# Hyena filter: two factors folded as one tile, stored by one transfer, all steps beside the first mixture's experts

## Chip, cores, metric

The kernel runs on one core of one Trainium2 chip. The metric is the device time of one execution in microseconds (us), taken as the median of several executions. Engines: PE (TensorE, matrix products), DVE (VectorE), ACT (ScalarE), POOL (GpSimd), SP (SyncE, which only issues transfers). Each engine takes its instructions strictly in the order in which they stand in its own program.

## What is computed

Two transformer blocks on 1024 tokens of width 1024. The first ends in a mixture of 32 experts. The second has a linear recurrence and a Hyena convolution side by side, and ends in a mixture of 16 experts. The filter of the Hyena convolution depends on weights alone and not on the tokens:

```python
h = jnp.sin(freq[0] * (z @ w1 + b1)); h = jnp.sin(freq[1] * (h @ w2 + b2))
h = (h @ w3).reshape(L, HYENA_ORDER, 2, HYENA_WIDTH)
filt = h * jnp.exp(-t * deltas[None, :])[:, None, None, :]
...
for n, gate in enumerate((x1, x2)):
    k = bidir_kernel(filt[:, n, 0], filt[:, n, 1])     # length 2L
    z = gate * fftconv(z, k, filt_bias[l, n])          # rfft(k) times rfft(z)
```

The kernel needs the spectrum of `k` for both orders `n` and all 1024 channels. It splits the transform of length 2L into two real halves, made from the sum and the difference of the two directions of the filter. These are the two factors, numbered `s` = 0, 1.

## The kernel before

The program runs in stages: first block (0 to about 700 us of the profiled execution), its mixture `moe1` (to about 1505), the start of the second block `start2` (to about 1585), the recurrence, the Hyena convolution, the output projections (to about 2790), the second mixture `moe2` (to the end). Code between stages is ordered ahead of time by a scheduler that may move an instruction past others of its engine; the rows below that show an order come from its result.

**moe1** (L731) runs 32 experts. Each needs six slabs of 1 MB of weights: `slab` (L643) loads one into one of four buffers `raw`, ACT rounds it to `hi` (L43), DVE subtracts to get `lo` (L44), and PE multiplies three times (L50 to L52: `hi*xh`, `lo*xh`, `hi*xl`). Every third expert multiplies its second matrix unsplit (L690, `rawn`). `fetch` gathers tokens `xg` by a POOL transfer (L634), `add` scales the result on ACT into `ys` (L740) and adds it to `h_d` in memory by a POOL transfer (L741). After each slab the function `tick` runs, 192 times in all, and each tick takes one step of the generator `fill`: that is the Hyena filter, put between the experts' instructions.

**filter_steps** (L964) has 16 rounds, one for each order `n` and each group `cg` of 128 channels, of 13 steps each, and one step ahead of them: 209. A round loads weights `W` through POOL (L983), forms sum and difference on POOL (L989, L990), splits them, multiplies with `H` on PE into `ps` (L1000, L1001), and DVE multiplies with the decay into `X0` and `X1`, one tile for each factor (L1002). Then for each factor in turn `fold_pairs` (L841) makes four `leaf` tiles on DVE by adds and subtracts (L847 to L863, 18 instructions), PE multiplies each with a constant `F` into `ks` (L1023), ACT copies `ks` to `kv` (L1029) after every second leaf, and POOL stores `kv` in `K_d` (L1031), 512 KB in runs of 512 bytes. `kv`, `ks` and `ps` have one buffer each, so the first copy into `kv` of a factor waits until the store of the factor before it has landed.

Ticks end before the steps do. The 17 steps that are left are taken up by the second block (`fl`, L1345); the scheduler puts their instructions into `start2`.

**start2** (L1149) loads eight row tiles `x` of the first block's result from `h_d` (L1156), five buffers of them (`XB`, L1116), squares and sums each twice on ACT (L1167, the second time after a product with `gf` on DVE, L1166), forms scales for four tiles at once, normalises to `n` (L1170), writes `x` times a scale to `x_d` (L1171 to L1173), transposes on PE (L92) and splits into `hTh` and `hTl`. With the first four tiles done, PE may multiply the first halves of two projections (L50 to L52 on `ps`, weights `whi` and `wlo` of a tile `wraw` loaded at L1125); the second halves need all eight tiles. From there on PE is busy nearly all the time through the recurrence.

Of the kernel before, what the change touches and what calls it, by code (L numbers as in the profile page):

```python
# [11 lines left out]
F32=mybir.dt.float32; F32R=mybir.dt.float32r; I32=mybir.dt.int32; U32=mybir.dt.uint32  # L12
AF=mybir.ActivationFunctionType; ALU=mybir.AluOpType; AX=mybir.AxisListType
PSUM=bass.MemoryType.PSUM; DRAM=bass.MemoryType.DRAM
# [65 lines left out]
def flat(ap):  # L80
    return ap.rearrange("p a b -> p (a b)")
# [372 lines left out]
CAP=96  # L454
# [275 lines left out]

def moe1(k,a,R,fill):  # L731

# [6 lines left out]
    def add(p,y,gate,idx):  # L739
        ys=p.tile([128,1024],F32,name="ys")[0:CAP]; nc.scalar.activation(ys,flat(y)[0:CAP],AF.Copy,scale=gate[0:CAP])  # L740
        nc.gpsimd.indirect_dma_start(out=acc_d,out_offset=bass.IndirectOffsetOnAxis(ap=idx[0:CAP],axis=0),in_=ys,in_offset=None,compute_op=ALU.add)  # L741
    with ExitStack() as es:
        wraw,whl,p=moe_pools(tc,es,2,"m1")
        R.route()
        ph,pt,py=psums(es,2)
        U=Unit(k,p,(ph,pt,py),wraw,whl,CAP)
        more=R.beyond(ph); k.gathers=[]
        def tick():
            if next(more,0)==0 and not U.wnat: U.wnat=es.enter_context(tc.tile_pool(name="m1x",bufs=2))
            next(fill,None)  # L750
        U.tick=tick; U.early=EARLY1
        ys_={}
        def unit(b):
            def down(h):
                ys_[b]=py.tile([128,2,512],F32,name="y")
                U.down(h,w2[b],ys_[b],True,True)
            def fin():
                add(p,ys_.pop(b),R.gw[:,b:b+1],R.tok[:,b:b+1])
            return dict(fetch=lambda: U.fetch(xn_d,R.tok[:,b:b+1]),up=lambda x: U.up(x,w1[b],w3[b],NAT(b)),down=down,fin=fin)
        us=[unit(b) for b in range(32)]  # L760
        run_units(U,us,2)

    nov=nc.values_load(R.nov[0:1,0:1],min_val=0,max_val=NB-32)
# [199 lines left out]
FC=128  # L963
def filter_steps(k,a,H_d,K_d,KN_d,p,pp):  # L964


    nc=k.nc
# [7 lines left out]
    for cg in range(1024//C):  # L975
# [3 lines left out]
        for n in range(2):  # L979
# [13 lines left out]
            yield  # L993
            Xs=[p.tile([128,8,C],F32,name=f"X{s}") for s in range(2)]
            for i in range(4):
                ps=pp.tile([128,2,2,C],F32,name="ps")
                for j in range(2):
                    t=2*i+j
                    with k.tc.issue_after(k.routed_pe.ins) if cg==n==t==0 else nullcontext():
                        nc.tensor.matmul(ps[:,j],H[:,128*t:128*t+128],Wh[:,0:2],start=True,stop=False)  # L1000
                    nc.tensor.matmul(ps[:,j],H[:,128*t:128*t+128],Wl[:,0:2],start=False,stop=True)  # L1001
                for s in range(2): nc.vector.tensor_tensor(Xs[s][:,2*i:2*i+2],ps[:,:,s],dec[:,2*i:2*i+2],op=ALU.mult)  # L1002
                if i%2: yield
# [4 lines left out]
            nc.tensor.matmul(ps[0:1,0],H[:,0:1],Wl[:,2],start=False,stop=True)  # L1008
            for s in range(2): nc.vector.tensor_tensor(Xs[s][0:1,0],ps[0:1,0],dec[0:1,0],op=ALU.mult)
            nc.vector.tensor_tensor(Xs[0][0:1,0],Xs[0][0:1,0],br,op=ALU.add)  # L1010
            for s in range(2):
                X=Xs[s]
                kv=p.tile([128,8,C],F32,name="kv")
                fold=fold_pairs(nc,p,X,C)
                nx=next(fold)
                yield
                for _ in range(4):
                    b,o=nx
                    nx=next(fold,None)
                    if b%4==0: ks=pp.tile([128,4,C],F32,name="ks")  # L1020
                    for j in range(2):
                        for q in range(2):
                            nc.tensor.matmul(ks[:,b%4+j],F[:,b+j,q,128*s:128*s+128],o[:,j,q],start=q==0,stop=q==1)  # L1023
                    if s==0 and b==0:
                        ps=pp.tile([128,4,C],F32,name="ps")
                        for q in range(2): nc.tensor.matmul(ps[0:1,0],FN[:,q:q+1],o[:,0,q],start=q==0,stop=q==1)
                        kn=p.tile([1,C],F32,name="kn"); nc.vector.tensor_copy(kn,ps[0:1,0])
                        nc.gpsimd.dma_start(KN_d[n,cg:cg+1],kn)
                    if b%4: nc.scalar.activation(kv[:,b-2:b+2],ks,AF.Copy)  # L1029
                    if b<6: yield  # L1030
                nc.gpsimd.dma_start(K_d[n,cg,:,:,s],kv)  # L1031
                yield
# [82 lines left out]
NPRE=3  # L1115
XB=5  # L1116

# [489 lines left out]
def net(tc, a, c, out):  # L1607
    k=K(); k.tc=tc; k.nc=tc.nc; k.c=c; nc=tc.nc
    with tc.tile_pool(name="const",bufs=1) as pc, tc.tile_pool(name="dram",bufs=1,space=DRAM) as k.dram:
# [8 lines left out]
        with tc.tile_pool(name="rt1",bufs=1) as po:  # L1618
# [5 lines left out]
            R,vec=k.R,k.vec  # L1624
            fl=filter_steps(k,a,H_d,K_d,KN_d,fls.enter_context(tc.tile_pool(name="fl",bufs=1,side="right")),fls.enter_context(tc.tile_pool(name="flp",bufs=1,space=PSUM)))
            moe1(k,a,R,fl)
        R,rt=block2(k,a,vec,h_d,K_d,KN_d,fl,fls.close,dict(x2=x2_d,ga=ga_d,sg=sg_d,ma=ma_d,z=z_d,x3=x3_d,xn2=xn2_d))
        moe2(k,a,R,out)
# [29 lines left out]
```

## Time and profile before

| | us |
|---|---|
| median of 3 runs | 3951.88 (3943.78 to 3955.34) |
| profiled execution, device time | 3954.99 |
| its span from first to last instruction | 3953.2 |
| busy: PE, DVE, ACT, POOL | 3707.7, 3079.9, 2215.5, 445.9 |
| mean granted clock of TensorE | 0.969 of full speed |

A view by windows gives the busy time of each engine in a stretch, with the granted clock (1.00 is 2.4 GHz, 0.50 is 1.2 GHz), the share of time in which the 16 DMA engines had a packet, and the rate. A timeline lists instructions with start, duration, engine, line, output and inputs, and in brackets how long the engine sat idle before and what it was then released by. PEld is the loading of weights into TensorE, which runs beside the products. Products overlap: 512 columns are issued every 0.23 us at the full clock, though one lasts 0.39.

### The profile page before, as it was taken

Reading aid. Unit: us, or ns where it says so; the run is one execution under the profiler, and the core shown is the slowest. Engines: PE = TensorE matmul, PEld = TensorE weight load, DVE = VectorE, ACT = ScalarE, POOL = GpSimd, SP = SyncE. Lnnn points to the kernel's source line nnn. Section 1 sums busy time; section 2 is a strip of 40 time slices with the busy share of each in tenths; the row PEclk is TensorE's granted clock in tenths of the full one; section 3 lists DMA queues with packets and bytes.
Section 4 is the critical chain, followed back from the end, with each engine's and each line's share of the span. In section 5 each row is a group of like instructions: output and inputs, shape, how many; then the busy total and the mean of one; then the engine's idle time right before and its main releaser. Section 6 shows DMA issues by size and latency. Waiting matters only on the chain.

```text
span 3953.2 us, 49738 instructions
## 1 busy us (share of the span) xinstructions
PE 3707.7 (94%) x18392; PEld 2955.4 (75%) x18392; DVE 3079.9 (78%) x4728; ACT 2215.5 (56%) x2522; POOL 445.9 (11%) x469
## 2 busy tenths in 40 slices
PE   8999898899989996999999999999699999999997
PEld 6787676577666674777888887877587778777785
DVE  3655765799888897676889999743788888888887
ACT  3733653566566664785333334222477777777776
POOL 0013000322333221100000000000000010100100
PEclk9999899899999997999999999999799999999998
DMA  3234635899989994122333335644799999999997
GB/s 97 67 94 110 168 98 177 279 333 317 312 289 305 321 297 144 58 84 85 102 96 107 110 105 157 201 139 170 259 373 378 374 367 380 368 373 375 366 383 297
DMA packets 459240, 900.99 MB, mean 228 GB/s; under 512 B 41734, under 2 KB 140257, under 8 KB 458610
## 3 DMA queue, kind: packets, MB, share of 16 engines
q1 hardware_dynamic: 414578, 801.90, 58.3%
q0 software_dynamic: 42832, 92.21, 8.5%
q10 hardware_dynamic: 1584, 3.67, 0.3%
q8 instruction: 146, 2.39, 0.3%
q14 instruction: 100, 0.82, 0.1%
HBM read 795.27 MB, written 102.29 MB: 227 GB/s over the span
## 4 chain that ended last, share of the span: by engine, by line
PE 60%; DVE 8%; issue 5%; ACT 5%; DMA 5%; POOL 1%; DVEq 0%; ACTq 0%; POOLq 0%; SPq 0%
PE h L51 7%; PE h L52 7%; PE h L50 7%; PE ps L51 5%; PE ps L52 5%; PE ps L50 5%; PE y L51 4%; PE y L52 3%; PE y L50 3%; PE iv L1086 3%; DVE lo L44 2%; DMA raw<-in_expert_w 2%; PE ks L1023 1%; PE U L1074 1%; PE y L690 1%
## 5 line engine op out<-in xcount | busy, mean ns | idle before, releaser
L44 DVE TENSOR_TENSOR lo<-raw,hi 128x2048 fp32r<-128x2048 f32 x551 | 1250.3, 2287 | 148.7 <-ACT hi L43 148.0
L43 ACT ACTIVATE hi<-raw 128x2048 fp32r<-128x2048 f32 x551 | 1047.9, 1913 | 210.7 <-PE h L52 114.3
L51 PE MATMUL h<-lo,xh 128*128 128x512 f32 (+1 forms) x1536 | 612.0, 398 | 14.2 <-DVE lo L44 13.5
L50 PE MATMUL h<-hi,xh 128*128 128x512 f32 (+1 forms) x1536 | 611.7, 399 | 0.7 <-ACT xh L43 0.7
L52 PE MATMUL h<-hi,xl 128*128 128x512 f32 (+1 forms) x1536 | 603.9, 393 | 0.0
L50 PE MATMUL ps<-hTh,whi 128*128 128x512 f32 x896 | 359.4, 402 | 3.3 <-ACT ge L1252 2.8
L51 PE MATMUL ps<-hTl,whi 128*128 128x512 f32 x896 | 355.3, 397 | 0.0
L52 PE MATMUL ps<-hTh,wlo 128*128 128x512 f32 x896 | 354.4, 396 | 0.0
L51 PEld LDWEIGHTS h<-lo,xh 128*128 128x128 f32 (+1 forms) x1536 | 276.8, 180 | 103.3 <-DVE lo L44 36.2
L52 PEld LDWEIGHTS h<-hi,xl 128*128 128x128 f32 (+1 forms) x1536 | 276.3, 180 | 71.4 <-issue 1.4
L50 PEld LDWEIGHTS h<-hi,xh 128*128 128x128 f32 (+1 forms) x1536 | 276.8, 180 | 69.9 <-ACT xh L43 1.2
L51 PE MATMUL y<-lo,hh 128*128 128x512 f32 (+1 forms) x680 | 272.0, 400 | 0.4 <-DVE lo L44 0.4
L50 PE MATMUL y<-hi,hh 128*128 128x512 f32 (+1 forms) x680 | 267.8, 394 | 0.3 <-ACT hi L43 0.3
L52 PE MATMUL y<-hi,hl 128*128 128x512 f32 (+1 forms) x680 | 266.8, 392 | 0.0
L44 DVE TENSOR_TENSOR wlo<-wraw,whi 128x1024 fp32r<-128x1024 f32 x96 | 117.2, 1221 | 131.7 <-ACT whi L43 104.4
L634 POOL DMA_INDIRECT xg<-xn_d,tok x48 | 101.5, 2115 | 862.0 <-issue 780.8
L50 PEld LDWEIGHTS ps<-hTh,whi 128*128 128x128 f32 x896 | 170.8, 191 | 37.3 <-ACT ge L1252 3.3
L52 PEld LDWEIGHTS ps<-hTh,wlo 128*128 128x128 f32 x896 | 170.4, 190 | 35.6
L51 PEld LDWEIGHTS ps<-hTl,whi 128*128 128x128 f32 x896 | 171.3, 191 | 33.3 <-DVE hTl L44 0.5
L43 ACT ACTIVATE whi<-wraw 128x1024 fp32r<-128x1024 f32 x96 | 101.4, 1056 | 161.2 <-PE ps L51 154.4
L1023 PEld LDWEIGHTS ks<-leaf,F 128*128 128x128 f32 x1024 | 139.0, 201 | 65.5 <-ACT kv L1029 30.5
L1023 PE MATMUL ks<-leaf,F 128*128 128x128 f32 x1024 | 145.0, 287 | 41.3 <-ACT kv L1029 26.3
(615 smaller groups left out, 7108.7 us busy)
## 6 DMA issues: line engine op xcount, KB each, us to landing
raw<-in_expert_w SPq DMA_DIRECT2D x170, 1024.0 KB
raw<-in_w_down SPq DMA_DIRECT2D x128, 1024.0 KB
raw<-in_w_up SPq DMA_DIRECT2D x127, 1024.0 KB
raw<-in_w_gate SPq DMA_DIRECT2D x126, 1024.0 KB
wraw<-in_w_in SPq DMA_DIRECT2D x80, 512.0 KB
K<-K_d SPq DMA_DIRECT2D x256, 128.0 KB
rawn<-in_expert_w SPq DMA_DIRECT2D x22, 1024.0 KB
K_d<-kv POOLq DMA_DIRECT2D x32, 512.0 KB, 6.9
```

The costliest lines, as they stand in the source:

```text
L43: nc.scalar.activation(hi, src, AF.Copy)
L44: (eng or nc.vector).tensor_tensor(lo, src, hi.bitcast(F32), op=ALU.subtract)
L50: nc.tensor.matmul(ps, sh, mh, start=start, stop=False)
L51: nc.tensor.matmul(ps, sh, ml, start=False, stop=False)
L52: nc.tensor.matmul(ps, sl, mh, start=False, stop=stop)
L634: s.k.gathers.append(s.k.nc.gpsimd.indirect_dma_start(out=xg,out_offset=None,in_=src_d,in_offset=bass.IndirectOffsetOnAxis(ap=idx[0:s.m],a ...
L690: for n in range(2): nc.tensor.matmul(y[0:s.m,n],hh[:,f],raw[:,j,512*n:512*n+512],start=first and f==0,stop=last and f==3)
L1023: nc.tensor.matmul(ks[:,b%4+j],F[:,b+j,q,128*s:128*s+128],o[:,j,q],start=q==0,stop=q==1)
L1074: for q in range(2): nc.tensor.matmul(U[:,j,q],F[:,2*(b+j)+q],um[:,j,q],start=True,stop=True)
L1086: for i in range(2): nc.tensor.matmul(iv[:,j,q].rearrange("p a t -> p (a t)"),Y[i][:,j,q],G[:,2*(b+j)+q,i],start=i==0,stop=i==1)
```

## The change

Both factors become halves of one tile `X` of twice the width, are folded by one call of `fold_pairs`, and each leaf's products for both factors go to one `ks`, copied to `kv` at once; one transfer of 1 MB, 8 KB for each partition, stores a round. A round has 8 steps instead of 13. `moe1` spreads all 129 steps over its first 190 ticks, so nothing is left for the second block. `ys` of the first mixture has one buffer instead of two; the row tiles of `start2` have eight instead of five; the folding has a pool of its own (`folds`).

```diff
 def add(p,y,gate,idx):
-        ys=p.tile([128,1024],F32,name="ys")[0:CAP]; nc.scalar.activation(ys,flat(y)[0:CAP],AF.Copy,scale=gate[0:CAP])
+        ys=p.tile([128,1024],F32,name="ys",bufs=1)[0:CAP]; nc.scalar.activation(ys,flat(y)[0:CAP],AF.Copy,scale=gate[0:CAP])
...
+        due=[0,0]
         def tick():
...
-            next(fill,None)
+            due[0]+=1
+            while due[1]*190<due[0]*nfill: next(fill,None); due[1]+=1
...
         run_units(U,us,2)
+        for _ in fill: pass
...
-            Xs=[p.tile([128,8,C],F32,name=f"X{s}") for s in range(2)]
+            X=p.tile([128,8,2,C],F32,name="X")
...
-                for s in range(2): nc.vector.tensor_tensor(Xs[s][:,2*i:2*i+2],ps[:,:,s],dec[:,2*i:2*i+2],op=ALU.mult)
+                nc.vector.tensor_tensor(X[:,2*i:2*i+2],ps,dec[:,2*i:2*i+2,None,:].to_broadcast([128,2,2,C]),op=ALU.mult)
...
-            for s in range(2):
-                X=Xs[s]
-                kv=p.tile([128,8,C],F32,name="kv")
-                fold=fold_pairs(nc,p,X,C)
...
-                    if b%4: nc.scalar.activation(kv[:,b-2:b+2],ks,AF.Copy)
-                    if b<6: yield
-                nc.gpsimd.dma_start(K_d[n,cg,:,:,s],kv)
+            kv=p.tile([128,8,2,C],F32,name="kv")
+            fold=fold_pairs(nc,folds(),X.rearrange("p t s c -> p t (s c)"),2*C)
+            nx=next(fold)
+            yield
+            for _ in range(4):
+                b,o=nx
+                nx=next(fold,None)
+                ks=pp.tile([128,2,2,C],F32,name="ks")
+                for j in range(2):
+                    for s in range(2):
                         for q in range(2):
+                            nc.tensor.matmul(ks[:,j,s],F[:,b+j,q,128*s:128*s+128],o[:,j,q,C*s:C*s+C],start=q==0,stop=q==1)
...
+                nc.scalar.activation(kv[:,b:b+2],ks,AF.Copy)
+                if b==6: nc.gpsimd.dma_start(K_d[n,cg],kv)
                 yield
...
-XB=5
+XB=8
...
-            moe1(k,a,R,fl)
-        R,rt=block2(k,a,vec,h_d,K_d,KN_d,fl,fls.close,dict(x2=x2_d,ga=ga_d,sg=sg_d,ma=ma_d,z=z_d,x3=x3_d,xn2=xn2_d))
+            moe1(k,a,R,fl,FSTEPS,lambda: ff.append(fls.enter_context(tc.tile_pool(name="flf",bufs=1,side="right"))))
+        fls.close()
+        R,rt=block2(k,a,vec,h_d,K_d,KN_d,iter(()),lambda: None,dict(x2=x2_d,ga=ga_d,sg=sg_d,ma=ma_d,z=z_d,x3=x3_d,xn2=xn2_d))
```

Three places in the engines' orders show what moves.

POOL in the middle of moe1. Before, one round of the filter has two stores `K_d<-kv`, with the gather `xg`, the addition to `h_d` and other rounds' `W` between them:

```order
L1031 DMA K_d_74<-kv_8538 1024x1x128
L741 DMA h_d_62<-ys_8756,tok_3840 1152x1024
L634 DMA xg_8985<-xn_d_63,tok_3840 96x1024
L1031 DMA K_d_74<-kv_8720 1024x1x128
L741 DMA h_d_62<-ys_8982,tok_3840 1152x1024
L634 DMA xg_9174<-xn_d_63,tok_3840 96x1024
L984 DMA br_9341<-in_filt_bias_2 1x16x8
L1028 DMA KN_d_75<-kn_9067 16x1x8
L1031 DMA K_d_74<-kv_9028 1024x1x128
```

After, at about the same place, two stores stand a whole round apart, each of 2048 numbers for a partition:

```order
L1035 DMA K_d_74<-kv_8281 128x2048
L995 TENSOR_TENSOR W_8910<-W_8910 128x128
L996 TENSOR_TENSOR W_8910<-W_8910 128x128
L741 DMA h_d_62<-ys_8628,tok_3840 1152x1024
L634 DMA xg_8844<-xn_d_63,tok_3840 96x1024
L990 DMA br_8911<-in_filt_bias_2 1x16x8
L1033 DMA KN_d_75<-kn_8736 16x1x8
L741 DMA h_d_62<-ys_8841,tok_3840 1152x1024
L989 DMA W_9294<-in_filt_w3_2 64x2x128
L634 DMA xg_9011<-xn_d_63,tok_3840 96x1024
L1035 DMA K_d_74<-kv_8674 128x2048
```

The store of the first factor is gone from between the factors; one remains for a round.

PE from the end of moe1 into start2. Before, products of the filter's last round stand behind the end of the mixture and ahead of the first transposes (L92):

```order
L1001 MATMUL ps_14857<-Wl_14439,H_6080 128x256
L1007 MATMUL ks_15051<-Wh_14438,H_6080 1x128
L1008 MATMUL ks_15051<-Wl_14439,H_6080 1x128
L1023 MATMUL ks_15070<-leaf_15061,F_6074 128x128 x4
L1026 MATMUL ps_15075<-leaf_15061,FN_6076 1x128 x2
L1023 MATMUL ks_15070<-leaf_15067,F_6074 128x128 x4
L1023 MATMUL ks_15102<-leaf_15086,F_6074 128x128 x4
L1023 MATMUL ks_15102<-leaf_15099,F_6074 128x128 x4
L1023 MATMUL ks_15126<-leaf_15117,F_6074 128x128 x4
L1023 MATMUL ks_15126<-leaf_15123,F_6074 128x128 x4
L92 MATMUL ps_13074<-ident_60,n_13070 128x128 x4
```

After, the transposes follow the mixture's last product and its loop at once:

```order
L52 MATMUL y_12565<-hi_12586,hl_12562 96x512
L773 REGISTER_ALU
L773 COMPARE_AND_BRANCH
L773 UNCONDITIONAL_BRANCH
L92 MATMUL ps_12716<-ident_60,n_12712 128x128 x4
```

The filter's products have moved ahead of the end of the mixture, among the experts' products.

SP at the start of start2. Before, the last three row tiles stand behind four weight tiles:

```order
L769 UNCONDITIONAL_BRANCH
L1156 DMA x<-h_d 128x1024 x4
L1125 DMA wraw<-in_w_in 128x8x128 x2
L1156 DMA x<-h_d 128x1024
L1125 DMA wraw<-in_w_in 128x8x128 x2
L1156 DMA x<-h_d 128x1024 x3
L1125 DMA wraw<-in_w_in 128x8x128 x4
```

After:

```order
L773 UNCONDITIONAL_BRANCH
L1160 DMA x<-h_d 128x1024 x4
L1129 DMA wraw<-in_w_in 128x8x128 x2
L1160 DMA x<-h_d 128x1024 x4
L1129 DMA wraw<-in_w_in 128x8x128 x6
```

All eight row tiles are now issued ahead of the third weight tile. From the first half projection on, the order of every engine is the same in both kernels.

## Rows read from the trace of the kernel before

**Rows 1.** Windows: stretch, length, busy us (instructions) by engine, PEclk, DMA share, GB/s.

```profile
745.00:1500.00 755.00, 717.59 (x3720) 515.44 (x3719) 658.44 (x981) 462.09 (x453) 221.16 (x177) 0.97 0.92 303
...
1508.00:1583.00 75.00, 41.90 (x192) 33.37 (x193) 54.13 (x113) 39.96 (x67) 13.44 (x26) 0.72 0.53 172
```

**Rows 2.** Waits of PE, 745 to 1505: us in total, times, longest.

```profile
PE ks L1023 <- ACT kv L1029: 23.3, 6, 9.0
```

**Rows 3.** Timeline in moe1: start, duration, instruction, idle before and releaser.

```profile
1123.60 10.05 POOL L634 DMA_INDIRECT xg<-xn_d,tok  x1 [0.30 <-issue]
1133.65 1.00 POOL L1031 DMA_DIRECT2D K_d<-kv  x1
1140.58 0.60 ACT L1029 ACTIVATE kv<-ks 128x512 f32<-128x512 f32 x1 [9.45 <-DMA K_d<-kv]
1141.23 2.08 PE L1023 MATMUL ks<-leaf,F 128*128 128x128 f32 x8 [8.43 <-ACT kv L1029]
...
1254.46 2.07 PE L1023 MATMUL ks<-leaf,F 128*128 128x128 f32 x8 [8.95 <-ACT kv L1029]
```

**Rows 4.** View of the tile K_d, its stores: time from issue to landing.

```profile
DMA to landing us min/median/max: 3.8/6.9/9.9
```

**Rows 5.** Windows behind three of the stalls, columns as in rows 1.

```profile
1030.00:1040.00 10.00, 9.96 (x40) 7.65 (x41) 4.77 (x6) 4.18 (x3) 0.00 (x0) 0.71 1.04 319
1140.00:1150.00 10.00, 8.77 (x31) 5.22 (x32) 2.76 (x2) 3.48 (x4) 1.05 (x3) 0.75 0.25 79
1250.00:1260.00 10.00, 5.54 (x24) 4.66 (x25) 2.76 (x2) 3.89 (x4) 1.59 (x1) 0.62 0.52 139
```

**Rows 6.** Groups on PE, 1499.8 to 1550: count, busy us, mean ns, idle before.

```profile
L1023 PE MATMUL ks<-leaf,F 128*128 128x128 f32 x96 | 17.1, 342 | 18.5 <-DVE leaf L863 10.1 <-DVE leaf L849 4.6 <-ACT kv L1029 3.6
```

**Rows 7.** Chain that ended last, 1440 to 1660: start, share in us, piece.

```profile
1486.86 0.89 PE ks L1023 x8
1487.75 0.53 PE ps L1026 x4
```

**Rows 8.** Waits of all engines, 800 to 1500.

```profile
POOL K_d L1031 <- ACT kv L1029: 93.6, 15, 12.2
...
ACT hi L43 <- DMA raw<-in_expert_w: 36.0, 18, 3.9
```

**Rows 9.** Timeline in start2, SP, ACT, DVE and PE, as in rows 3.

```profile
1507.86 2.07 SPq L1156 DMA_DIRECT2D x<-h_d  x4
1524.45 1.06 ACT L43 ACTIVATE whi<-wraw 128x1024 fp32r<-128x1024 f32 x1 [5.44 <-DMA wraw<-in_w_in]
1543.33 1.28 DVE L1170 SCALAR_TENSOR_TENSOR n<-x,rby,gm 128x1024 f32<-128x1024 f32 x1
1548.71 7.61 SPq L1156 DMA_DIRECT2D x<-h_d  x3
1569.45 1.29 DVE L1170 SCALAR_TENSOR_TENSOR n<-x,rby,gm 128x1024 f32<-128x1024 f32 x1
1582.47 1.22 PE L50 MATMUL ps<-hTh,whi 128*128 128x512 f32 x2
```

**Rows 10.** Groups on DVE by shape, 1508 to 1550, columns as in rows 6.

```profile
L1166 DVE TENSOR_TENSOR x<-x,gf 128x1024 f32<-128x1024 f32 x5 | 6.1, 1221 | 1.3 <-ACT junk L1167 0.8 <-issue 0.5
L44 DVE TENSOR_TENSOR hTl<-ps,hTh 128x512 fp32r<-128x512 f32 x3 | 2.0, 684 | 0.0
```

**Rows 11.** Groups on DVE by shape, 745 to 1507: the folding.

```profile
L858 DVE SCALAR_TENSOR_TENSOR S<-DE,X 128x512 f32<-128x512 f32 x59 | 40.0, 678 | 0.1
L861 DVE SCALAR_TENSOR_TENSOR UW<-S 128x128 f32<-128x128 f32 x118 | 28.6, 279 | 0.2
```

**Rows 12.** View of the line of the addition to h_d: issue to landing.

```profile
DMA to landing us min/median/max: 5.4/8.6/14.7
```

**Rows 13.** Timeline of one such addition and the next ys, as in rows 3.

```profile
1118.45 4.85 POOL L741 DMA_INDIRECT h_d<-ys,tok  x1 [3.86 <-ACT ys L740]
1150.64 1.11 ACT L740 ACTIVATE ys<-y,gw 96x1024 f32<-96x1024 f32 x1 [1.12 <-PE y L690]
```

More of the change, by code (lines that the diff above doesn't have):

```diff
@@ L729, in moe_pools, with moe1 @@
     return e(name=pre+"r",bufs=nr if nb>1 else 2),e(name=pre+"w",bufs=3*SPL if nb>1 else 2*SPL),e(name=pre,bufs=nb)
-def moe1(k,a,R,fill):
+def moe1(k,a,R,fill,nfill,folds):
     tc,nc=k.tc,k.nc
@@ L746, in moe1 @@
         U=Unit(k,p,(ph,pt,py),wraw,whl,CAP)
+        folds()
+        due=[0,0]
         more=R.beyond(ph); k.gathers=[]
@@ L963, with filter_steps @@
 FC=128
-def filter_steps(k,a,H_d,K_d,KN_d,p,pp):
+FSTEPS=1+16*8
+def filter_steps(k,a,H_d,K_d,KN_d,p,pp,folds):
     nc=k.nc
@@ L1008, in filter_steps @@
             nc.tensor.matmul(ps[0:1,0],H[:,0:1],Wl[:,2],start=False,stop=True)
-            for s in range(2): nc.vector.tensor_tensor(Xs[s][0:1,0],ps[0:1,0],dec[0:1,0],op=ALU.mult)
-            nc.vector.tensor_tensor(Xs[0][0:1,0],Xs[0][0:1,0],br,op=ALU.add)
-            for s in range(2):
-                X=Xs[s]
-                kv=p.tile([128,8,C],F32,name="kv")
-                fold=fold_pairs(nc,p,X,C)
[L1015 to L1021, printed above, removed]
-                        for q in range(2):
[L1023 to L1028, printed above, removed]
-                    if b%4: nc.scalar.activation(kv[:,b-2:b+2],ks,AF.Copy)
-                    if b<6: yield
-                nc.gpsimd.dma_start(K_d[n,cg,:,:,s],kv)
@@ new lines, in filter_steps @@
+            for s in range(2): nc.vector.tensor_tensor(X[0:1,0,s],ps[0:1,0],dec[0:1,0],op=ALU.mult)
+            nc.vector.tensor_tensor(X[0:1,0,0],X[0:1,0,0],br,op=ALU.add)
+            kv=p.tile([128,8,2,C],F32,name="kv")
[8 more added lines that the diff above has]
+                    for s in range(2):
+                        for q in range(2):
+                            nc.tensor.matmul(ks[:,j,s],F[:,b+j,q,128*s:128*s+128],o[:,j,q,C*s:C*s+C],start=q==0,stop=q==1)
+                if b==0:
+                    ps=pp.tile([128,4,C],F32,name="ps")
+                    for q in range(2): nc.tensor.matmul(ps[0:1,0],FN[:,q:q+1],o[:,0,q,0:C],start=q==0,stop=q==1)
+                    kn=p.tile([1,C],F32,name="kn"); nc.vector.tensor_copy(kn,ps[0:1,0])
+                    nc.gpsimd.dma_start(KN_d[n,cg:cg+1],kn)
+                nc.scalar.activation(kv[:,b:b+2],ks,AF.Copy)
+                if b==6: nc.gpsimd.dma_start(K_d[n,cg],kv)
@@ L1624, in net @@
             R,vec=k.R,k.vec
-            fl=filter_steps(k,a,H_d,K_d,KN_d,fls.enter_context(tc.tile_pool(name="fl",bufs=1,side="right")),fls.enter_context(tc.tile_pool(name="flp",bufs=1,space=PSUM)))
-            moe1(k,a,R,fl)
-        R,rt=block2(k,a,vec,h_d,K_d,KN_d,fl,fls.close,dict(x2=x2_d,ga=ga_d,sg=sg_d,ma=ma_d,z=z_d,x3=x3_d,xn2=xn2_d))
+            ff=[]
+            fl=filter_steps(k,a,H_d,K_d,KN_d,fls.enter_context(tc.tile_pool(name="fl",bufs=1,side="right")),fls.enter_context(tc.tile_pool(name="flp",bufs=1,space=PSUM)),lambda: ff[0])
+            moe1(k,a,R,fl,FSTEPS,lambda: ff.append(fls.enter_context(tc.tile_pool(name="flf",bufs=1,side="right"))))
+        fls.close()
+        R,rt=block2(k,a,vec,h_d,K_d,KN_d,iter(()),lambda: None,dict(x2=x2_d,ga=ga_d,sg=sg_d,ma=ma_d,z=z_d,x3=x3_d,xn2=xn2_d))
         moe2(k,a,R,out)
```

## Prediction

> **What bounds the kernel now.** I read the windows first, then the waits of PE, then single stalls in the timeline. In the first mixture, from 745 to 1500 us, PE is busy for 717.6 of 755 us and DVE for 658.4 [rows 1]: PE sets the pace, so what PE is given or spared there moves the end, and DVE, 13% idle, does not. Of the 37.4 us in which PE stands still there (755 - 717.6), 23.3 belong to one wait, the products `ks` waiting for ACT's copy `kv` of the products before them [rows 2]. The reader is to see that this is no slow copy. At 1141 PE has stood still for 8.43 us, ACT for 9.45, and ACT was released by a transfer: the store of `kv` to `K_d`, which POOL had issued at 1133.65, since a gather of 10.05 us was ahead of it in POOL's queue; at 1254 the same, with 8.95 us [rows 3]. The store of the first factor has to land before the second factor may use `kv`, and landing takes 6.9 us at the median [rows 4]. Behind three of the stalls the granted clock is 0.71, 0.75 and 0.62 in the next 10 us [rows 5], that is, part of them at the lower level of 1.2 GHz, though PE is at work again.
>
> From 1508 to 1583 nothing is a full bound: PE is busy for 41.9 of 75 us, DVE for 54.1, ACT for 40.0 [rows 1]. It is a chain of loads, sums, scales and transposes with the rest of the filter in between. From 1582 PE runs steadily, so the start of the second half projection at 1582.47 [rows 9] is the point to watch: all that comes behind it is ordered alike in both kernels and moves with it.
>
> **The change part by part.** First, the wait for the store between the factors goes. After the change the store is issued behind the last of a round's four leaves, and the next copy into `kv` belongs to the first leaf of the next round. By the order of PE's products, at 0.23 us for each of 512 columns, 20 to 27 us of other products lie between the two, against 2 to 6 before. Even a store that POOL issues 10 us late and that lands in 9.9 us, the longest [rows 3, 4], fits. So I take the whole wait out, 23.3 us [rows 2]. Bounds: 0 to 23.3.
>
> Second, the clock behind the stalls. At a granted clock c, a stretch with PE busy for b holds b x (1 - c) us too many: 9.96 x 0.29 + 8.77 x 0.25 + 5.54 x 0.38 = 2.9 + 2.2 + 2.1 = 7.2 us [rows 5]. If PE does not stop, this goes too. Bounds: 0 to 7.2.
>
> Third, PE's work that is moved into the mixture. Behind 1500 stand 96 passes of `ks` [rows 6]; eight take 0.89 us at the full clock [rows 7], so 96 take 10.7. With them go 14 products of `H` with 256 columns (half of the 0.23 us for 512, 1.7 us in all) and four passes with `FN`, 0.53 us [rows 7]. PE is the bound there, so all 12.9 us count. There is no cover for them.
>
> Fourth, the wider instructions of DVE. 128 numbers take 0.279 us, 512 take 0.678 [rows 11], so a number costs 0.00104 us and an instruction 0.146 beside. A round drops 22 instructions (4 of the decay, 18 of the folding), 3.2 us by this price, some 50 us in 16 rounds; less the last round that moves in (about 15 us of DVE), DVE is relieved by 35 us of 658. I credit nothing, as DVE is not the bound. If it shortened PE's other 14 us of standing still, the end would come up to 14 us earlier: that is the lower bound. `kv` keeps four copies of 512 numbers a round, so ACT has the same work.
>
> Fifth, the weights. PE's stalls let the four weight buffers fill. ACT still waits for weights 18 times, 36.0 us in all [rows 8], so the transfers are near their limit: 303 GB/s at a DMA share of 0.92 [rows 1]. A shorter mixture asks for about 2% more each second. I charge 3 us, between 0 and 17 (all that the first three parts gain). The stores carry the same bytes; that a store now writes 8 KB in one run is left uncredited.
>
> Sum of the mixture: -23.3 - 7.2 + 12.9 + 3 = -14.6 us.
>
> Sixth, `start2`. Time 0 is SP's issue of the row tiles, 1507.86 [rows 9]. The first normalisation comes at 1543.33. ACT, in order, sat 5.44 us for the first weight tile until 1524.45 [rows 9], and this stays; what leaves are the filter's copies on ACT and its folds on DVE behind it. Going through ACT's and DVE's new orders with the durations of before, from 1524.45: roundings and squares of 1.06 us [rows 9] (one width, 1024 numbers), products of 1.22 [rows 10], and an estimate of 4 us for the column instructions, I get the first normalisation at 1539.7, 3.6 us earlier. The second group of four then starts at 1569.45 in the trace, 26.1 us after the first, because the last three row tiles are issued at 1548.71 only, when a buffer is free [rows 9]. With eight buffers they are there in time, and DVE's own work is the limit between the two: 4 normalisations of 1.28 [rows 9], 8 splits of 0.684 and 3 products of 1.22 [rows 10], and 2 scalings with 15 column instructions, estimated at 4.5 us as they are shorter: 5.1 + 5.5 + 3.7 + 4.5 = 18.8 us, 7.3 less. Against that, the first half projections, which before ran while DVE waited, now stand between the transposes of the second group on PE; I charge 1 us. Sum -3.6 - 7.3 + 1 = -9.9; bounds -4 (the first part alone) and -14 (the clock, 0.72 on the mean there [rows 1], rises as well).
>
> Together -14.6 - 9.9 = -24.5, taken as -25 us. Against the profiled execution's 3955.0 that is 3930; that execution lies 3.1 us above the median of the runs, 3951.9, so for the median I take 3927.
>
> One rule speaks against this change, since `ys` goes from two buffers to one and `kv` stays at one. First the rows: an addition to `h_d` lands 8.6 us after its issue at the median and 14.7 at most [rows 12], and the next `ys` comes 32 us after the issue in rows 13, and about 23 after the change (740 us for 32 experts). So one buffer costs nothing. The Trainium skill, "Trainium Kernel Development and Optimization", section "Best Practices", says to double-buffer so that transfers overlap with compute; by it each of these stores would be exposed. No run here shows that yet, and the last rival prices it.
>
> **The rivals.** (a) The stalls go, but the weights become the bound and take most of it back. For it: ACT's 36 us of waits for weights [rows 8]. Against: the DMA engines still stand empty for 8% of the mixture [rows 1], and three of PE's stalls are stalls of the weights' queue too, at 79 and 139 GB/s behind two of them [rows 5]. The mixture then gains about 2 us, `start2` 10: 3940.
>
> (b) The wait stays, because POOL's queue holds the one store back for more than 20 us, with gathers of 10 us [rows 3] and sums of `W` ahead of it. Then the mixture only has more work, +12.9, and `start2` gains 9.9: +3, about 3955, no change. Against: 15 times from 800 to 1500 POOL stood idle for `kv` ahead of a store, 93.6 us in all [rows 8]; so it is mostly early, not late.
>
> (c) More goes than I credit: PE's other stalls shrink with DVE's relief, and the weights cost nothing. -25 - 3 - 14 gives some 3910; half of it 3918.
>
> (d) Slower: `ys` with one buffer holds ACT, and behind ACT the rounding of the next slab, and so PE. It decides when issue and landing of an addition exceed the 23 us of an expert. POOL's own time for one reached 4.85 us [rows 13] and landing 14.7 [rows 12], 19.5 together in the worst case, so it is close. If the 1 MB stores made it typical at 25 us, 31 experts would wait 2 us each: +62 - 25, about 3989.
>
> **How the numbers follow.** The forecast, 3927 with a range of its own from 3914 to 3940, has 0.62. (a) has 0.13, (b) 0.11, (c) beyond 3914 0.08, (d) 0.06. A measurement of this kernel can tell about 0.3%, 12 us, from no change: faster is below 3940.0, slower above 3963.7. Faster: nearly all of the forecast (0.60), (c) 0.08 and half of (a), 0.06, give 0.74. The same: the rest of the forecast, half of (a), nearly all of (b), 0.19. Slower: (d) and a little of (b), 0.07. The range for 8 in 10 leaves out (d), most of (b) and the ends of (c): 3906 to 3948.
>
> **What would show it.** In the trace after, PE's waits for `kv` should be under 4 us in the mixture, and no wait of ACT should name the store of `K_d`; the clock should show no 10 us below 0.8 there except behind a late slab. The mixture, from its first slab to the last `y`, should be 10 to 20 us shorter although it holds 16 whole rounds. ACT's wait for weights should stay below 50 us (else a). `ys` should never wait for a transfer (else d). The second normalisation group should start some 19 us after the first, and the second half projection some 65 us after SP's first row tile instead of 74.6. I am wrong if PE's idle time in the mixture does not fall below 25 us, or if the gain of `start2` is given back behind 1583, where the orders are the same.

## The result, and the profile after

The change makes the kernel slower: 3974.92 us at the median of 8 runs, against 3950.05 us for the kernel before on the same chip. The ratio is 1.0060, with a 95% interval from 1.0049 to 1.0070. The forecast was 3927, with a range from 3906 to 3948; the time lies 27 us above the range's upper end.

The profiled execution after has a span of 3979.2 us, 26.0 more than the one before. To find where they come from I cut both spans at marks that both kernels have: PE's last products of the routing (`tb`, L565), POOL's issue of the third addition to `h_d`, that of the last but one, and SP's first load of a row tile in `start2`. "Start", "stretch", "tail" and "rest" below are the pieces between these marks and the end of the span. Each row is a window: its length, then busy us (instructions) of PE, PE's weight loads, DVE, ACT, POOL, then PE's granted clock, the DMA share and GB/s. First the kernel before:

```profile
694.18:808.31 114.13, 98.97 (x506) 70.87 (x507) 93.98 (x156) 63.88 (x70) 34.41 (x28) 0.89 0.85 284
808.31:1492.28 683.97, 649.60 (x3382) 469.51 (x3381) 601.20 (x885) 425.20 (x414) 201.30 (x163) 0.98 0.93 306
1492.28:1507.86 15.58, 12.26 (x60) 7.55 (x59) 7.83 (x22) 2.31 (x3) 4.37 (x3) 1.00 0.47 86
```

and the kernel after:

```profile
697.42:830.85 133.43, 102.20 (x511) 74.62 (x512) 96.98 (x127) 64.61 (x71) 40.52 (x26) 0.83 0.74 251
830.85:1535.83 704.98, 666.62 (x3499) 480.35 (x3498) 596.00 (x629) 435.90 (x425) 195.48 (x153) 0.98 0.89 298
1535.83:1550.23 14.40, 6.87 (x16) 2.29 (x15) 0.00 (x0) 1.11 (x1) 2.96 (x2) 0.89 0.40 65
```

The sum: start +19.3, stretch +21.0, tail -1.2, rest 2429.0 - 2445.3 = -16.3, and +3.2 that lie ahead of the first mark, where the two programs do the same; together 26.0. So `start2` gave more than forecast, and the whole loss is the first mixture, +39.1 where I had -14.6. In the stretch PE is busy for 17.0 us more, of which 12.9 are the moved work that the sum had, and idle for 38.4 instead of 34.4. DVE has 256 instructions fewer there, and nothing is shorter for it. The prediction was to be wrong if PE's idle time in the mixture did not fall below 25 us, and it did not.

The waits of PE in the mixture after (us in total, times, longest) answer to [rows 2]:

```profile
PE ps L1006 <- DVE X L1008: 22.1, 7, 4.6
PE ks L1028 <- ACT kv L1034: 12.7, 2, 11.9
PE pt L641 <- issue: 10.0, 1, 10.0
PE ps L1006 <- ACT Wh L43: 5.4, 1, 5.4
```

and before, over the same piece:

```profile
PE ks L1023 <- ACT kv L1029: 23.3, 6, 9.0
PE ps L1000 <- DVE X L1002: 6.4, 5, 3.1
PE pt L641 <- issue: 6.1, 1, 6.1
```

The wait for the store is gone as forecast, and other waits stand in its place. PE's products `ps` wait 22.1 us for `X` instead of 6.4. The 12.7 us that still name `kv` are nearly all one wait of 11.9 at the start, and that one is not the store's. ACT's waits show the other side; the first line answers to [rows 8]:

```profile
ACT hi L43 <- DMA raw<-in_expert_w: 73.8, 30, 7.4
...
ACT Wh L43 <- POOL W L996: 22.4, 2, 14.2
```

Before, over the same piece, ACT waited 21 times and 41.9 us for weight slabs, and once, 7.5 us, for `W`. The timeline of the start, POOL, DVE, ACT and PE (start, duration, instruction, idle before and its releaser):

```profile
739.16 1.32 POOL L989 DMA_DIRECT2D W<-in_filt_w  x2
...
745.29 2.27 DVE L44 TENSOR_TENSOR lo<-raw,hi 128x2048 fp32r<-128x2048 f32 x1
...
746.59 7.55 POOL L995 TENSOR_TENSOR W<-W 128x128 f32<-128x128 f32 x1 [5.60 <-DMA W<-in_filt_w]
752.55 1.27 DVE L867 SCALAR_TENSOR_TENSOR leaf<-UW,S 128x512 f32<-128x512 f32 x2
753.75 0.18 DVE L618 TENSOR_TENSOR tb<-tb,h 96x48 f32<-96x48 f32 x1
754.11 0.44 POOL L996 TENSOR_TENSOR W<-W 128x128 f32<-128x128 f32 x1
...
754.58 0.52 ACT L43 ACTIVATE Wh<-W 128x384 fp32r<-128x384 f32 x1 [14.24 <-POOL W L996]
...
756.81 0.58 ACT L1034 ACTIVATE kv<-ks 128x512 f32<-128x512 f32 x1
...
757.44 1.86 PE L1028 MATMUL ks<-leaf,F 128*128 128x128 f32 x7 [11.92 <-ACT kv L1034]
...
816.09 7.04 POOL L995 TENSOR_TENSOR W<-W 128x128 f32<-128x128 f32 x1 [8.05 <-DMA W<-in_filt_w]
823.09 0.44 POOL L996 TENSOR_TENSOR W<-W 128x128 f32<-128x128 f32 x1
...
823.57 0.52 ACT L43 ACTIVATE Wh<-W 128x384 fp32r<-128x384 f32 x1 [8.20 <-POOL W L996]
```

The load of the second round's `W` is issued at 739.16, and its two sums on POOL run from 746.59 to 754.55. ACT, in order, stands before the split of `W` for 14.24 us; the copy `kv` is behind it in its queue, and PE's next `ks` is behind `kv`. Some 6.3 us of ACT's wait are the load, and 8.0 are the sums. The first sum lasted 7.55 us and the second 0.44, though they are of one size: all through the first one DVE worked without a gap, from 745.29 to 753.93. In the third round ACT waits 8.20 us, and 7.4 of these are the sums.

`start2` after, SP and DVE, answers to [rows 9]:

```profile
1550.23 1.89 SPq L1160 DMA_DIRECT2D x<-h_d  x4
...
1580.30 1.28 DVE L1174 SCALAR_TENSOR_TENSOR n<-x,rby,gm 128x1024 f32<-128x1024 f32 x1
...
1598.73 1.28 DVE L1174 SCALAR_TENSOR_TENSOR n<-x,rby,gm 128x1024 f32<-128x1024 f32 x1
...
1611.27 0.73 PE L50 MATMUL ps<-hTh,whi 128*128 128x512 f32 x2 [0.57 <-ACT hTh L43]
```

The first normalisation comes 30.1 us after the first load (35.5 before), the second group 18.4 us after the first (26.1), the second half projection runs without a break from 61.0 us (74.6).

### The profile page after: what moved, and what is told of

The parts are those of the page before. It is cut to its first block, busy times and chain, and to the rows that moved or that the text cites. A ratio compares the mean times of both kernels' runs of the same rounds, so it can differ in the third digit from the quotient of the medians.

```text
span 3979.2 us, 49273 instructions
## 1 busy us (share of the span) xinstructions
PE 3706.9 (93%) x18392; PEld 2951.6 (74%) x18392; DVE 3053.1 (77%) x4376; ACT 2222.1 (56%) x2528; POOL 441.5 (11%) x453
## 3 DMA queue, kind: packets, MB, share of 16 engines
q1 hardware_dynamic: 414578, 801.90, 57.5%
## 4 chain that ended last, share of the span: by engine, by line
PE 72%; DVE 10%; DMA 7%; ACT 5%; issue 5%; POOL 0%; SPq 0%; DVEq 0%; POOLq 0%; ACTq 0%
PE h L51 8%; PE h L52 7%; PE h L50 7%; PE ps L51 7%; PE ps L52 7%; PE ps L50 7%; PE y L51 3%; PE y L52 3%; PE y L50 3%; DMA raw<-in_expert_w 3%; DVE lo L44 3%; PE iv L1090 3%; PE ks L1028 2%; PE U L1078 1%; PE y L690 1%
## 5 line engine op out<-in xcount | busy, mean ns | idle before, releaser
L51 PE MATMUL h<-lo,xh 128*128 128x512 f32 (+1 forms) x1536 | 611.5, 398 | 13.0 <-DVE lo L44 12.4
L50 PE MATMUL ps<-xTh,whi 128*128 128x512 f32 x400 | 159.2, 399 | 0.1
L51 PE MATMUL ps<-xTl,whi 128*128 128x512 f32 x400 | 157.3, 393 | 0.3 <-DVE xTl L44 0.3
```

The source lines that it names most:

```text
L50: nc.tensor.matmul(ps, sh, mh, start=start, stop=False)
L51: nc.tensor.matmul(ps, sh, ml, start=False, stop=False)
```

## Experiments

Every kernel was timed beside the kernel before. In the table "gap" is the median of the kernel minus that of the kernel before on its chip; the pieces are those of the profiled execution, in us. A piece comes from a single execution, and a difference of a few us in one piece is within what two executions differ by: PE's wait that the profile calls "issue" ahead of the first `pt` is about 6 or about 10 us in kernels whose code there is the same. after_xb5, whose edit lies behind the mixture, repeats the start and the stretch of the kernel after to 0.1 and 3.7 us. The whole times of one kernel spread further: the kernel before ran from 3936.97 to 3961.60 us over all these runs.

| kernel | median | gap | ratio, 95% | start | stretch (PE busy) | rest |
|---|---|---|---|---|---|---|
| before | 3950.05 | 0 | 1 | 114.1 | 684.0 (649.6) | 2445.3 |
| after | 3974.92 | +24.9 | 1.0060, 1.0049-1.0070 | 133.4 | 705.0 (666.6) | 2429.0 |
| move_two | 3952.62 | +3.3 | 1.0004, 0.9991-1.0016 | 119.9 | 690.9 (660.9) | 2430.2 |
| move_kv2 | 3942.13 | -7.2 | 0.9975, 0.9964-0.9987 | 121.8 | 678.9 (657.2) | 2427.2 |
| move_lump | 3982.21 | +33.3 | 1.0089, 1.0069-1.0109 | 120.8 | 722.2 (665.1) | 2431.9 |
| kv2_lump | 3942.44 | -5.3 | 0.9988, 0.9977-0.9999 | 122.1 | 680.2 (656.7) | 2432.2 |
| before_half | 3938.22 | -10.7 | 0.9970, 0.9959-0.9982 | 117.7 | 663.4 (643.8) | 2447.3 |
| half_pre | 3934.28 | -13.4 | 0.9963, 0.9952-0.9975 | 114.2 | 662.0 (643.7) | 2446.5 |
| move_half_pre | 3935.67 | -9.9 | 0.9974, 0.9959-0.9989 | 115.4 | 677.1 (656.1) | 2430.6 |
| after_fine | 3940.60 | -8.8 | 0.9978, 0.9966-0.9989 | 123.8 | 677.5 (659.7) | 2428.5 |
| fine_split | 3942.66 | -6.3 | 0.9976, 0.9963-0.9989 | 122.7 | 676.3 (658.8) | 2432.3 |
| fine_pre | 3937.23 | -10.5 | 0.9975, 0.9966-0.9985 | 109.1 | 681.5 (659.9) | 2426.1 |
| fine_pace | 3963.86 | +14.0 | 1.0035, 1.0020-1.0050 | 126.4 | 696.8 (663.2) | 2431.0 |
| after_split | 3959.29 | +9.9 | 1.0024, 1.0008-1.0039 | 130.8 | 692.5 (662.7) | 2431.5 |
| after_pre | 3953.75 | +6.0 | 1.0017, 1.0006-1.0028 | 113.3 | 696.6 (664.1) | 2430.1 |
| pre_split | 3948.32 | +2.7 | 1.0003, 0.9990-1.0015 | 111.4 | 692.2 (662.9) | 2434.7 |
| after_gap | 3980.01 | +34.4 | 1.0074, 1.0059-1.0088 | 120.7 | 719.6 (674.8) | 2430.4 |
| after_pace | 3959.81 | +10.0 | 1.0026, 1.0012-1.0039 | 129.1 | 687.5 (660.6) | 2428.1 |
| after_xb5 | 3987.71 | +38.8 | 1.0091, 1.0070-1.0111 | 133.5 | 701.3 (665.5) | 2442.4 |

The profiled execution of fine_pre is the fastest of its twelve, so its pieces add up to less than its median.

**Undoing the fold.** The first theory was that steps which hold twice DVE's work delay the splits of weight slabs ("lumps"); the rivals were the 1 MB store ("burst") and that the mixture has no room for two more rounds ("full"). move_two keeps the two-factor code of before and makes the rest of the change, except that `ys` keeps its two buffers:

```
-            next(fill,None)
+            due[0]+=1
+            while due[1]*190<due[0]*nfill: next(fill,None); due[1]+=1
...
+        for _ in fill: pass
...
-            moe1(k,a,R,fl)
+            moe1(k,a,R,fl,209)
...
-XB=5
+XB=8
```

> The fold is undone: two factors, two tiles, two stores of 512 KB and 209 steps as in the kernel before, but all 209 spread over the 190 calls and finished beside the experts, with x buffers 8. Theory 'lumps' (129 steps that each hold twice the DVE work delay the split of the next weight slab, so that loads start late; after: ACT waited 73.8 us for weights instead of 41.9, PE 22.1 us for X instead of 6.4): X waits under 10 us, weights under 55 us, kv waits back at 20 to 25 us; the last addition of the mixture about 15 us later than before (the moved PE work), then 16 us won in start2, so about 3950 us. Theory 'burst' (stores of 1 MB, landing in 10.1 us at the median instead of 6.9, hold back the slabs): the same 3950. Theory 'full' (the mixture has no room for two more rounds whatever their form): 3970 to 3980.

It came to +3.3 us, and the x loads start 11.5 us later after the first mark than before. So "full" is out: the same work beside the experts costs 11 us there, not 39. Of the 25 us, some 22 come with the fold and what it does to steps and stores. One thing came otherwise than expected: PE's wait for `kv` did not return to 20 us or more but was 10.3, with nothing but the spacing of the steps changed there.

**The wait for the store alone.** Two kernels take it away without a fold. move_kv2 is move_two with `kv` in two buffers and `ys` in one; before_half is the kernel before with `kv` in halves, two buffers and 64 stores of 256 KB:

```
+                        kv=p.tile([128,4,C],F32,name="kv",bufs=2); nc.scalar.activation(kv,ks,AF.Copy)
+                        nc.gpsimd.dma_start(K_d[n,cg,:,b-2:b+2,s],kv)
```

> As move_two, with the wait of kv for its store taken away by a second kv buffer (room for it from ys, single as in the kernel after). The prediction's own term for that wait was 23.3 us, bounds 0 to 23.3. Theories 'lumps' and 'burst': kv waits under 3 us and 15 to 23 us under move_two, so 3927 to 3935. Theory 'full': the waits turn into waits for weights and X, less than 8 us under move_two. If ys with one buffer costs, ACT waits for a transfer ahead of ys.

> The kernel before with kv in halves of four blocks, two buffers of the same 4 KB in all, each stored by itself (64 stores of 256 KB): it takes away the wait of the next kv for the store and nothing else. The prediction's term was 23.3 us of waits and 7.2 of clock behind them, so 3920 to 3930 by it; by what move_kv2 gave against move_two (10.5 us): 3937 to 3942. If the extra stores hold POOL's queue as much as they free: 3948 to 3951.

Both gave about 10.5 us at the median (3.3 to -7.2, and -10.7). before_half came out by its second account and not by the 30.5 of the prediction; move_kv2 lies between its accounts. The two do not say the same: in move_two the wait was 10.3 us long, so there the gain is as long as the wait, and in the kernel before it was 23.3. The stretch of before_half, and its waits of PE over the mixture:

```profile
810.23:1473.66 663.43, 643.77 (x3382) 465.01 (x3381) 601.20 (x885) 424.76 (x414) 219.15 (x188) 0.99 0.95 316
```

```profile
PE ps L1000 <- DVE X L1002: 13.3, 7, 4.2
PE pt L641 <- issue: 10.6, 1, 10.6
...
PE ks L1022 <- ACT kv L1029: 2.7, 3, 1.2
```

The wait for `kv` falls from 23.3 to 2.7 us, the same 3382 products take 5.8 us less of PE (649.6 to 643.8, at a granted clock of 0.99 instead of 0.98), and the stretch is 20.5 us shorter. But waits for `X` doubled (6.4 to 13.3), the start was 3.6 us longer, and the rest 2.0.

**Lumps.** after_fine cuts a round of the kernel after into 13 steps instead of 8, with the same wide instructions (its fold hands over between the pieces of a leaf as well); move_lump and kv2_lump take the steps of move_two and move_kv2 two at a time:

```
-FSTEPS=1+16*8
+FSTEPS=1+16*13
...
+            next(fold)
+            yield
             nx=next(fold)
             yield
...
                 for j in range(2):
+                    if j: yield; nx=next(fold,None)
```

```
-            while due[1]*190<due[0]*nfill: next(fill,None); due[1]+=1
+            while due[1]*190<due[0]*nfill: next(fill,None); next(fill,None); due[1]+=2
```

> The kernel after with the same wide operations and the same single store, but a round cut into 13 steps instead of 8 (209 in all): pieces of the fold and the two blocks of a pair stand in steps of their own. 'lumps': X waits fall from 22.1 to under 10 us, ACT's wait for weights from 73.8 to under 55, the time to 3935 to 3955. 'burst' and 'full': no change, 3970 to 3980.

> move_two with its 209 narrow steps taken two at a time: 105 lumps in the 190 calls, each with about the DVE work of a step of the kernel after. 'lumps': PE's X waits over 15 us (move_two 7.9), ACT's wait for weights over 65 us (55.2), the stretch from third to last-but-one addition 700 to 708 us (690.9), and 3962 to 3973 us. Rival 'wide' (not the sum of a step counts but that each operation is wide, so nothing changes with narrow ones): 3949 to 3957 us, X waits under 10.

> move_kv2 (two factors, narrow operations, second kv buffer) with its steps taken two at a time. In move_lump the loss of 29.6 us came with waits of kv for its store (32.6 us) and not with those that 'lumps' had named, so this run has the lumps without that wait. 'lumps': still 10 us or more over move_kv2, 3952 to 3965, with waits for X and weights up. If lumps cost only by the store's wait: 3938 to 3946.

after_fine came to -8.8 us, as "lumps" wanted, and move_lump to +33.3, which is 9 us beyond the range of "lumps". But move_lump lost by another wait than expected. Its waits of PE in the stretch:

```profile
PE ks L1025 <- ACT kv L1031: 32.6, 7, 11.8
PE h L51 <- DVE lo L44: 6.2, 7, 2.0
PE ps L1002 <- DVE X L1004: 5.4, 3, 2.1
```

That is the store again, with even less between the factors. kv2_lump has the lumps without that wait, and there they cost nothing that can be told apart (-5.3 against -7.2). So the theory fell: in that kernel large steps alone do not slow the mixture.

**The store.** after_split sends it in two, fine_split the same with the fine steps:

```
-                if b==6: nc.gpsimd.dma_start(K_d[n,cg],kv)
+                if b%4==2: nc.gpsimd.dma_start(K_d[n,cg,:,b-2:b+2],kv[:,b-2:b+2])
```

> The kernel after with its store in two transfers of 512 KB, one after blocks 2 and 3 and one after 6 and 7. 'burst': landing back near 6.9 us at the median, ACT's wait for weights under 55 us, 3950 to 3960. 'lumps' and 'full': within 4 us of the kernel after, 3971 to 3979.

> after_fine with the store in two transfers of 512 KB. In the kernel after the split gave 15.6 us. If the large store costs by itself: 3924 to 3932 us. If it costs only where slabs are late anyway: 3936 to 3942.

15.0 us less (24.9 to 9.9) in the one, in the time that "burst" had named, though ACT's wait for weights stayed at 70.0 us where it wanted under 55; no gain in the other (-8.8 to -6.3). So the large store does not cost in every setting.

**The start.** after_pre issues each round's load of `W` half a round early, and moves its two sums on POOL to near the end of the round before; fine_pre and half_pre do so to fine_split and before_half, pre_split to after_split:

```
+            m=2*cg+n+1
+            if m<16: W,br=load(m//2,m%2)
             yield
...
+                if b==4 and m<16: adds(W,m//2,m%2)
```

> The kernel after with each round's load of W (2 transfers and the bias) issued in the middle of the round before, and the two sums on POOL near its end, instead of in the step that splits W. If the start of the mixture is late because ACT stands at the split of W with kv behind it (14.2 and 8.2 us; PE 11.9 and 5.4): these waits under 4 us and 12 to 18 us less than the kernel after, 3957 to 3963. If what follows then waits instead: 3968 to 3976.

> fine_split with the early load of W as in after_pre. ACT's waits for W there are 8.6 and 6.3 us at the start, PE's behind them 2.5 and 4.6: 4 to 8 us less, 3934 to 3939. Rival: POOL waits for W ahead of a gather, 3942 to 3946.

> before_half with the early load of W. The kernel before had one such wait (ACT 7.5, PE 3.9 us): 2 to 5 us less than before_half, 3933 to 3936. Rival as in fine_pre: 3938 to 3942.

> The kernel after with both mendings that helped it alone: W loaded half a round early (21 us less) and the store in two transfers (16 us less). If they mend different losses (the start, and the rest of the mixture): 3936 to 3942. If both mend the same one: 3950 to 3955.

after_pre is 18.9 us better than the kernel after (24.9 to 6.0), a little more than expected. Its start:

```profile
699.36:812.61 113.25, 96.92 (x512) 70.37 (x513) 93.17 (x125) 64.87 (x71) 29.21 (x26) 0.90 0.85 286
```

20.2 us shorter than after's, as long as before's, and no wait of PE names `kv` or `Wh` there any more. That half of the loss is shown to be the way of `W` to its split. The run moves the load and the sums together, so it does not part them; the rows of the kernel after give the sums the larger share, 15.4 of ACT's 22.4 us. In the others the early load gave 4.2 us (fine_pre) and 2.7 (half_pre) at the median, but their ratios of 0.9975 and 0.9963 do not stand clear of 0.9976 and 0.9970 without it. pre_split came out between its two accounts: by the medians the two mendings gave 18.9 and 15.0 us alone and 22.2 together, and in the stretch 8.4 and 12.5 alone and 12.8 together.

**The stretch.** In the kernel after, the six longest waits of PE for `X` began 11 to 17 us after a store was issued, with a late slab between. One of them, on POOL, ACT and PE:

```profile
1390.72 0.60 POOL L1035 DMA_DIRECT2D K_d<-kv  x1
...
1402.69 1.91 ACT L43 ACTIVATE hi<-raw 128x2048 fp32r<-128x2048 f32 x1 [7.30 <-DMA raw<-in_expert_w]
...
1407.58 0.58 PE L1006 MATMUL ps<-Wh,H 128*128 128x256 f32 x1 [4.62 <-DVE X L1008]
```

The slab is late for ACT by 7.30 us, DVE's half of its split stands ahead of `X` in DVE's queue, and PE waits for `X`. after_gap moves `X` away from the store with two empty steps a round:

```
             with k.tc.issue_after(k.routed.ins) if cg==n==0 else nullcontext(): split(nc,Wh,Wl,W[:,0:3])
             yield
+            yield
+            yield
```

> The kernel after with two empty steps in each round, between the split of W and the first products with H (161 steps over the same 190 calls, nothing else). In the kernel after every PE wait for X of 2.7 us or more ends 11 to 17 us after the 1 MB store of the round before was issued, behind a slab that came late. If it is this meeting of store, late slab and X products that costs: X waits from 22.1 to under 10 us, the stretch from third to last-but-one addition from 705 to 685 to 693 us, 3957 to 3964 us. If the slabs are late whatever stands behind the store: the waits turn up elsewhere, the stretch at 698 or more, 3970 to 3978.

The waits for `X` fell to 11.1 us and the stretch grew to 719.6: other waits took their place. So taking that meeting away does not take the loss away. Last, the same two kernels at another pace, 176 instead of 190 in the line that spreads the steps:

> The kernel after with its 129 steps spread over 176 calls instead of 190: the same lumps and stores, each round 7% sooner, so that stores and steps meet the slabs at other places. If the loss between third and last-but-one addition belongs to the form of the steps: the stretch stays at 700 to 712 us (705.0), 3970 to 3980 us. If it is how stores and slabs happen to meet: the stretch moves by 8 us or more either way.

> after_fine with its 209 steps over 176 calls. If the fine steps are robust: the stretch stays within 6 us of 677.5 and the time at 3936 to 3946. If after_fine was a lucky meeting: 685 us or more, 3948 or more.

The stretch of after_pace and that of fine_pace:

```profile
828.77:1516.22 687.45, 660.64 (x3481) 474.94 (x3480) 596.98 (x627) 430.51 (x420) 171.26 (x152) 0.99 0.91 307
```

```profile
820.04:1516.83 696.79, 663.17 (x3481) 479.73 (x3480) 595.10 (x625) 431.66 (x422) 217.70 (x149) 0.98 0.90 302
```

A round that comes 7% sooner makes the one 17.5 us shorter and the other 19.3 longer, and their times change places with it (+24.9 to +10.0, -8.8 to +14.0). So the loss of the stretch is not a fixed property of the large steps, nor is after_fine's gain one of the fine steps; at 190 calls after_fine was lucky and the kernel after unlucky. What is left is where stores, loads, additions and slabs happen to meet, which no run takes apart. In fine_pace one such meeting can be read, on POOL, DVE, ACT and PE; it makes 10.78 of the 19.3 us:

```profile
1126.02 22.09 POOL L741 DMA_INDIRECT h_d<-ys,tok  x1 [0.30 <-issue]
...
1142.24 4.47 DVE L44 TENSOR_TENSOR lo<-raw,hi 128x2048 fp32r<-128x2048 f32 x2
...
1156.93 1.11 ACT L740 ACTIVATE ys<-y,gw 96x1024 f32<-96x1024 f32 x1 [12.29 <-DMA h_d<-ys,tok]
...
1159.06 0.90 PE L641 MATMUL pt<-ident,xg 96*128 96x96 f32 x4 [10.78 <-DVE xl L44]
```

POOL's addition takes 22.09 us, in which DVE has no gap before 1146.71; the single `ys` comes free only when it has landed, ACT waits 12.29 us for that, and PE stands behind ACT.

**x buffers.** after_xb5 is the kernel after with `XB=5`.

> The kernel after with 5 x buffers as before, so that the last three row tiles of the second group load late again. By the prediction XB is worth 7.3 us: second group's first normalisation 59 to 63 us after the first x load (48.5 with 8, 61.6 before), time 3980 to 3984. If what follows waits for weights anyway: within 3 us of the kernel after.

It costs 13.9 us more (24.9 to 38.8), beyond the 5 to 9 expected, and the second group:

```profile
1573.91 1.28 DVE L1174 SCALAR_TENSOR_TENSOR n<-x,rby,gm 128x1024 f32<-128x1024 f32 x1
...
1601.21 1.28 DVE L1174 SCALAR_TENSOR_TENSOR n<-x,rby,gm 128x1024 f32<-128x1024 f32 x1
```

starts 27.3 us after the first and 57.5 after the first load (1543.72), 9.0 more than with eight buffers.

**What beats both.** half_pre, two factors with `kv` in halves and `W` loaded early, has the lowest median: 3934.28 us, ratio 0.9963 (0.9952 to 0.9975). The intervals of several others overlap with it.

> The sum of what helped with two factors: kv in halves, W loaded early, all steps beside the experts, x buffers 8. From the profiles: half_pre's time up to the x loads plus the 11.4 us that the move cost in move_two, and the 2430 us that follow them in move_two instead of 2446: 3925 to 3932. Rival: the moved rounds fill the mixture again and it comes out as half_pre, 3932 to 3937.

move_half_pre comes out level with it, as its rival had said: the stretch is 15.1 us longer for the moved rounds, and the rest 15.9 shorter for the row tiles.

## Why the prediction was wrong, point by point

**The bound** was read right: PE sets the pace of the mixture. The step that failed is the sum over it, -14.6 us where +39.1 came. It took the wait for the store with its clock out in full (-30.5), and left every other meeting as it stood in the trace of before, that is, put them at nothing. The runs showed two things in its place. ACT's waits for `W` at the start, which it had no term for, cost 18.9 us by after_pre. In the stretch the freed time came back as other waits, and another pace alone moves it by 17 to 19 us. The terms on the side of loss, 12.9 and 3, were too few.

**First, the wait for the store** (-23.3, bounds 0 to 23.3): gone in the kernel after, where ACT's wait table names no store. Its worth, measured alone in before_half, is 10.7 us at the median, with the clock behind it, so the term was mis-sized. Part of what PE no longer waited for `kv` it waited for `X`.

**Second, the clock** (-7.2): about right where the stalls alone are removed, 5.8 us of PE in before_half. In the kernel after it did not come: less the 12.9 of moved work, PE is busy in the stretch for 4.1 us more than before, and the start ran at 0.83 instead of 0.89.

**Third, PE's moved work** (+12.9): right. PE is busy for 12.4 us more in the stretch of move_half_pre than in that of half_pre, and the stretch is 15.1 longer.

**Fourth, DVE's relief** (0 credited): right not to, though its size was wrong. From the first mark to the row tiles DVE is busy for 693.0 us instead of 703.0, 10.0 less and not 35. The 0.146 us beside the numbers is not all DVE's time: two instructions in a row overlap, as the `leaf` of 0.676 us each that take 1.27 together. Nothing is shorter for it.

**Fifth, the weights** (+3, bounds 0 to 17): ACT's wait for slabs rose by 32 us. As a cost of its own it is not shown: over the stretch these waits are 66.4 us in the kernel after and 47.9 in after_xb5, with the same mixture, and the stretches are 705.0 and 701.3.

**What the sum lacked** is the way of `W` to its split: a load and two sums on POOL, in the same step as the split that needs them. The change redraws when that step comes, and what DVE does meanwhile. The trace of before has the same wait once (ACT 7.5 us, PE 3.9), and I gave it no term: 18.9 us by after_pre.

**Sixth, `start2`** (-9.9, bounds -4 to -14): the right direction, too small; -16.3 in the profile. The first normalisation gained 5.4 us (3.6 forecast). The second group came 18.4 us after the first (18.8). But eight buffers were worth 13.9 us and not 7.3: without them the second group comes 9.0 us later, and the rest is 13.4 us longer (2442.4 to 2429.0). What the 4.4 us behind the second group are is open.

**The rivals.** Slower had a chance of 0.07, by (d) and a little of (b), and came by neither. (a) came nearest in kind, but it had the mixture 2 us shorter and not 39.1 longer. (b) did not come: no copy waited for the store. (d) did not decide the kernel after: `ys` waited for no transfer there, with additions that land in 9.4 us at the median and 17.0 at most, which answers to [rows 12]. Its mechanism exists, as fine_pace shows with 12.29 us, once in 32 experts. The rule of the Trainium skill, "Trainium Kernel Development and Optimization", section "Best Practices", to double-buffer so that transfers overlap with compute, agrees for `kv` with the 10.7 us of before_half, and for `ys` with that one wait in fine_pace; in the kernel after the single `ys` made no wait.

**What stays open** is which meetings make the stretch 705.0 us in the kernel after and 677.5 in after_fine. The runs speak against large steps by themselves (kv2_lump), the large store by itself (fine_split) and the meeting of store and `X` (after_gap). Each was read at one spacing only, and the runs show that a change of pace alone moves the stretch by 17 to 19 us either way.

## What to carry to other kernels

When a step of background work is moved or cut anew, list its loads as well as its instructions, and see who stands in line behind the first user of each load: here a load of 128 KB and two sums on POOL, in the step that needed them, cost 19 us. In a stretch where the bound engine, the weights and the helpers are all near their limit, the worth of a removed wait can be less than its length (10.7 us for a wait of 23.3 in before_half, though 10.5 for one of 10.3 in move_kv2), and another spacing of the same work can move the time by as much as the edit (14.9 and 22.8 us here): test the edit at two paces before believing its sign. The row tiles loaded ahead, a gain at a clean hand-over, were the one part here that gave more than forecast.

## What the runs showed of the hardware that I had not expected

An addition to `h_d` that POOL issues in 1.6 us at the median took it 22.09 us once in fine_pace, and one landed 30.8 us after its issue, against 17.0 at most in the kernel after. The line of fine_pace in the view of the tile `h_d`:

```profile
DMA to landing us min/median/max: 5.1/9.9/30.8
```

POOL's long instructions fall together with DVE's work. Spans on POOL are rough, but the 96 sums of `W` in the mixtures of the kernels before, after and fine_pace took 0.44 to 8.39 us, and less the time in which DVE ran an instruction that reads two tiles in SBUF (`lo`, `leaf`, `S`, `UW`, `DE`), at most 0.84 us are left of any of them. Of the gathers `xg` there at most 1.01 us are left, of the additions at most 1.99. The gather of 10.05 us that held back the store in [rows 3] is such a case: DVE had no gap from 1117.75 to 1132.79. The stores `K_d`, issued on POOL as well, took 1.5 us at most. That DVE's work is what holds POOL is read from these rows; no run was made to show it.
